# The memory's features through the weight stream, an eight-wide first group, and a first piece in halves

## The chip, the cores and the metric

One of the eight cores of a Trainium2 chip runs the kernel. The metric is device microseconds (us) from launch to end, median of the runs. The core has TensorE (PE, matrix products), VectorE (DVE), ScalarE (ACT) and GpSimd (POOL), which each take their instructions in order, and SyncE (SP), which here issues DMA transfers, in order too. ACT and POOL also issue some transfers. Sums of products build up in eight banks of PSUM.

## What is computed

One decoder layer for 320 tokens (256 of a prompt and 8 x 8 of a second group), width 2048, float32:

```
p = x @ w_in                       # 2048 -> 43 column tiles of 128
u_x, u_gate, u_rwkv = split(p)     # RG-LRU block and RWKV-7 mixer (16 heads of 64, state S)
mix = concat(rg_lru(conv(u_x)) * gelu(u_gate), rwkv7_mix(u_rwkv)) @ w_out
mem_k = mem @ xa_wk ; mem_v = mem @ xa_wv      # 256 memory tokens
x = LN(ALPHA*x + mix)
x = LN(ALPHA*x + softmax((x @ xa_wq) @ mem_k^T) @ mem_v @ xa_wo)
x = LN(ALPHA*x + relu(x @ mlp_w1)**2 @ mlp_w2)
```

mem_k, mem_v and the states of both mixers are outputs as well.

## The kernel before

Every float32 operand is split into a high and a low part (h and l), and a product of a 128x128 weight tile with activations takes three matmuls: h by aH, h by aL, l by aH. One such set is called a triple here. Weights are stored in the order of use, as pieces of 128x1024 float32 (512 KB) with eight weight tiles each. The class `Stream` brings them: `load` issues the DMA of a piece on SP into one of 3 buffers `wraw`, `conv` casts it on ACT into `wh` (4 buffers), and `poll` subtracts on DVE, `wl` = `wraw` - `wh` (4 buffers); when a subtraction is written out, the next load is too. `get(i)` keeps up to three pieces cast ahead.

Activations are split in the same way, one 128-row k-tile at a time, by `Act.put` (one cast on ACT, one subtraction on DVE) into units `u0` to `u7`: even units hold the high parts of four k-tiles, odd ones the low parts. x (16 k-tiles of 128x320) is in u0 to u7 during the input projection. The memory features (16 k-tiles of 128x256) get the same units afterwards, so that a unit of theirs is free only when the last products with the four k-tiles of x in it are done.

`linear` runs a projection over groups of column tiles. In a group that is g tiles wide, a piece holds 8/g k-tiles for each of the g tiles; the groups of w_in (`G_IN`) are one of 4 tiles, then 37 of one, then one of 2. w_in's column tiles come in the order c0 c1 c2 (codes), then r, k, v (RWKV-7), x, g (RG-LRU) of pair 0, of pair 1, and so on to pair 7. After a tile the function `on_win` reads the PSUM bank and may start or end a task. The 8 tasks ("rwkv", i) and the 8 tasks ("lru", i) are Python generators with many small steps. When the program is written, a planner (`Sched`) lays their steps between the triples by a cost model of its own; the order that comes out is fixed. `sch.drain(name)` writes out what is left of a task at once, with the steps of other tasks that come due, and no triples between:

```
elif kind == "x":
    ...
    sch.drain(("lru", i - 1))
    sch.add(lru_task(i, ue), ("lru", i), 1.0)
```

In an RWKV task PE first computes sums for the normalised keys (`t,KM` and `qn,K`). DVE then makes the operands `AR` and `BK` in seven instructions, here called the block (with a reciprocal in it), PE multiplies them (`AR,BK`), DVE masks the result into `GM`, POOL brings `GM` through DMA into `bm`, inverts small triangular matrices in 30 multiplications and additions (`tt`, `Xp`), and sends the result through DMA (`bx`) as `Xn`, which the products `Xn,GM` on PE need. Then come the scan steps with the state (`R`, `UV`, `S`, `XT`).

The memory's features were loaded by SP as 16 transfers of 128 KB (`t<-in_mem`, L1122), three quarters while the last group of w_in runs (the argument `last` of `linear`), the fourth when the projection `wk` has begun. `wk` is in groups of two tiles. After each of its tiles, `on_k` copies PSUM to a buffer on ACT, and POOL issues two stores of it (`mk`, L1132, and `out_mem_k`, L1133).

At the start x_tile loads the k-tiles of x, 160 KB each, on SP, and a piece of w_in after every second one.

Of the kernel before, what the change touches and what calls it, by code (L numbers as in the profile page):

```python
# [119 lines left out]
class Sched:  # L120
# [169 lines left out]
class Stream:  # L290


    def __init__(self, nc, sch, A, tt, raw, hp, lp, srcs, ahead_conv):
        self.nc, self.sch, self.A, self.tt = nc, sch, A, tt
        self.raw, self.hp, self.lp = raw, hp, lp
        self.srcs = srcs
# [20 lines left out]
    def load(self):  # L317
        k = self.n_load
        t = self.raw.tile([128, 1024], F32, name="wraw")
        self.nc.sync.dma_start(t, self.srcs[k])  # L320
        self.r[k] = t
        self.n_load += 1

    def conv(self):
        k = self.n_conv
        t = self.r.pop(k)
        h = self.hp.tile([128, 1024], F32R, name="wh")
        l = self.lp.tile([128, 1024], F32R, name="wl")
        cur, self.sch.cur = self.sch.cur, None
        self.A.copy(h, t)  # L330
        self.sch.cur = cur
        self.pend.append((k, t, h, l, self.sch.free["A"]))
        self.c[k] = (h, l)
        self.n_conv += 1

    def get(self, i):
        while self.n_load < min(len(self.srcs), self.n_low + 3):
            self.load()
        while self.n_conv < min(self.n_load, i + 1 + min(i, self.ac)):
            self.conv()  # L340
        self.poll(i)
        return self.c.pop(i)


def body(ctx, tc, I, O):
# [113 lines left out]
    class Act:  # L459
# [80 lines left out]
    with ExitStack() as mx_ctx:  # L540
# [25 lines left out]
        def tmp(n=NTOK):  # L566
            return tp.tile([128, 348], F32, name="t")[:, :n]
# [106 lines left out]
        def rwkv(p, zr, zk, zv):  # L674
# [140 lines left out]
            for c in range(4):  # L815
# [19 lines left out]
                yield PE_FH  # L835
# [132 lines left out]
        def sample(p, S0, AR, XT, GM, B4, UV, PT, res):  # L968
# [21 lines left out]
            yield PE_HH  # L990
# [741 lines left out]
```

## Time and profile before

| | before |
|---|---|
| median of 3 runs | 2037.86 us (2033.55 to 2039.96) |
| profiled execution, own time | 2038.85 us |
| its span, first to last instruction | 2036.8 us |
| mean granted TensorE clock | 0.985 |
| PE busy | 1978.4 us |
| DVE, ACT, POOL busy | 1056.1, 894.4, 434.1 us |

The input projection runs from 6.65 us to about 460 us of the span, wk from there to about 608 us, the rest is behind. In rows of the timeline the first number is the start in us, the second how long the row's instructions took, "xN" how many there are, and a bracket gives the idle time of that engine just before, with what ended it. The granted clock is a share of TensorE's 2.4 GHz, so 0.5 is the lower of its levels, 1.2 GHz.

### The profile page before, as it was taken

How to read it: one execution, taken by the hardware profiler on the slowest of the kernel's cores; microseconds unless marked ns; L12 is line 12 of the kernel's file. 1: busy time of each engine (PE TensorE's matmuls, PEld its weight loads, DVE VectorE, ACT ScalarE, POOL GpSimd, SP SyncE). 2: the span in 40 equal slices, each digit the busy share in tenths (PEclk: the TensorE clock that was granted, in tenths of full speed). 3: DMA queues.
4: the chain of work that ended last, by engine and by line, in shares of the span. 5: the costliest groups of instructions: out<-in, count | busy, mean ns of one | idle time of the engine just before them, and what ended most of it. 6: DMA issues, size and time to landing. Idle time of an engine off the chain costs nothing.

```text
span 2036.8 us, 38079 instructions
## 1 busy us (share of the span) xinstructions
PE 1978.4 (97%) x15750; PEld 1883.3 (92%) x15750; DVE 1056.1 (52%) x1654; ACT 894.4 (44%) x1464; POOL 434.1 (21%) x661
## 2 busy tenths in 40 slices
PE   7999999988999999999999999999999999999996
PEld 7998888877898999988899999999999999999996
DVE  5676767755545446444476434443444344433444
ACT  5565565555435335544334543334333342234333
POOL 0143023332311345322154310001000010001133
PEclk9999999998999999999999999999999999999998
DMA  7453343344557764787643444444444444444442
GB/s 238 140 154 94 108 119 117 120 125 132 167 184 245 242 215 144 258 316 279 253 144 116 156 154 145 154 147 152 149 151 149 148 153 147 154 146 154 145 149 90
DMA packets 103149, 333.82 MB, mean 164 GB/s; under 512 B 13808, under 2 KB 23824, under 8 KB 102976
## 3 DMA queue, kind: packets, MB, share of 16 engines
q1 hardware_dynamic: 86688, 278.68, 43.1%
q0 software_dynamic: 16288, 52.72, 7.8%
q8 instruction: 123, 2.02, 0.4%
q14 instruction: 50, 0.41, 0.1%
HBM read 315.66 MB, written 15.65 MB: 163 GB/s over the span
## 4 chain that ended last, share of the span: by engine, by line
PE 93%; DMA 2%; DVE 2%; ACT 1%; issue 1%; POOL 1%; SPq 0%; POOLq 0%; ACTq 0%; DVEq 0%
PE ps L284 93%; DMA t<-in_mem 1%; DMA wraw<-in_w_in 1%; POOL u L284 0%; DVE u L284 0%; DVE wl L284 0%; DMA t<-in_x 0%; ACT u L284 0%; ACT wh L284 0%; DVE t L284 0%; POOL r L284 0%; DMA Xn<-bx 0%; DVE S L284 0%; ACT L284 0%; POOL wl L284 0%
## 5 line engine op out<-in xcount | busy, mean ns | idle before, releaser
L284 DVE TENSOR_TENSOR wl<-wraw,wh 128x1024 fp32r<-128x1024 f32 x494 | 612.5, 1243 | 569.3 <-ACT wh L284 568.8
L284 ACT CAST wh<-wraw 128x1024 fp32r<-128x1024 f32 x502 | 525.7, 1048 | 645.5 <-PE ps L284 577.5
L284 PE MATMUL ps<-u,wh 128*128 128x320 f32 (+1 forms) x3424 | 761.6, 313 | 14.1 <-ACT u L284 13.3
L284 PE MATMUL ps<-r,wh 128*128 128x320 f32 x3072 | 680.9, 310 | 2.1 <-ACT r L284 1.8
L284 PEld LDWEIGHTS ps<-u,wh 128*128 128x128 f32 x3424 | 571.6, 191 | 31.2 <-ACT u L284 13.8
L284 PE MATMUL ps<-u,wl 128*128 128x320 f32 (+1 forms) x1712 | 526.4, 307 | 0.0
L284 PEld LDWEIGHTS ps<-r,wh 128*128 128x128 f32 x3072 | 514.8, 188 | 7.0 <-issue 3.8
L284 PE MATMUL ps<-r,wl 128*128 128x320 f32 x1536 | 475.6, 310 | 0.0
L284 PEld LDWEIGHTS ps<-u,wl 128*128 128x128 f32 x1712 | 326.4, 191 | 0.0
L284 PEld LDWEIGHTS ps<-r,wl 128*128 128x128 f32 x1536 | 289.3, 188 | 0.0
L284 PE MATMUL ps<-h,wh 128*128 128x320 f32 x1024 | 225.6, 309 | 0.0
L284 POOL TENSOR_TENSOR r<-r 128x320 f32<-128x320 f32 x64 | 46.0, 721 | 721.0 <-ACT r L284 721.0
L284 PEld LDWEIGHTS ps<-h,wh 128*128 128x128 f32 x1024 | 170.9, 188 | 0.2
L284 PE MATMUL ps<-h,wl 128*128 128x320 f32 x512 | 158.2, 309 | 0.0
L284 DVE TENSOR_TENSOR u<-u,ps 128x320 f32<-128x320 f32 x134 | 61.6, 484 | 80.6 <-PE ps L284 77.9
L284 ACT ACTIVATE r<-ps 128x320 f32<-128x320 f32 x64 | 28.0, 438 | 157.7 <-PE ps L284 157.7
L284 PEld LDWEIGHTS ps<-h,wl 128*128 128x128 f32 x512 | 96.1, 188 | 0.0
L284 POOL TENSOR_TENSOR s<-s,u 128x320 f32<-128x320 f32 x42 | 66.0, 1571 | 91.5 <-DVE u L284 91.1
L284 PE MATMUL ps<-wh,u 128*128 128x512 f32 x256 | 79.9, 391 | 0.0
L284 ACT ACT_TABLE_LOAD x50 | 64.2, 1283 | 9.1 <-DVE mxs L284 7.6
L893 POOL DMA_DIRECT2D bm<-GM x16 | 10.9, 685 | 241.2 <-DVE GM L284 241.2
L284 PEld LDWEIGHTS ps<-wh,u 128*128 128x128 f32 x256 | 48.1, 188 | 10.0
(245 smaller groups left out, 1625.5 us busy)
## 6 DMA issues: line engine op xcount, KB each, us to landing
wraw<-in_w SPq DMA_DIRECT2D x256, 512.0 KB, 3.5
wraw<-in_w_in SPq DMA_DIRECT2D x86, 512.0 KB, 4.0
wraw<-in_wk SPq DMA_DIRECT2D x32, 512.0 KB, 3.7
wraw<-in_wv SPq DMA_DIRECT2D x32, 512.0 KB, 3.9
wraw<-in_w_out SPq DMA_DIRECT2D x32, 512.0 KB, 4.2
kv<-in_cache_k POOLq DMA_DIRECT2D x32, 512.0 KB, 6.7
wraw<-in_wq SPq DMA_DIRECT2D x32, 512.0 KB, 4.6
kv<-in_cache_v POOLq DMA_DIRECT2D x32, 512.0 KB, 9.1
```

What stands on the lines that cost most here:

```text
L284: r = f(*a, **k)
L893: nc.gpsimd.dma_start(blocks(bm[b], h), GM[HS[1 - h], h, :, 0, :])
```

## The change

The first group of w_in is eight tiles wide (c0 to g0), so a piece there holds one k-tile, and the group has all eight PSUM banks. The memory's features come as four pieces of 512 KB through `Stream`, which casts and subtracts them right into the units (`Act.quarter`), in the order quarter 0, quarter 1, wk piece 0, quarters 2 and 3, wk piece 1 and so on. Piece 0 of w_in is loaded as two halves, by ACT's queue and by SP's, and is cast and subtracted in halves; from the second k-tile of x on a piece is loaded after each k-tile, until three are on the way. The stores `mk` and `out_mem_k` are issued by SP. `PE_HH(0)` and `PE_FH(0)` tell the planner that these steps need no new PSUM bank.

```
--- before.py
+++ after.py
@@ -45,7 +45,7 @@
     return g
 
 
-G_IN = _groups(len(WIN_TILES) - 2, 4) + [(len(WIN_TILES) - 2, 2)]
+G_IN = _groups(len(WIN_TILES) - 2, 8) + [(len(WIN_TILES) - 2, 2)]
 G_SQ = _groups(16, 4)
 G_V = [(0, 4), (4, 4), (8, 4), (12, 4)]
 G_1 = _groups(16, 1)
@@ -290,10 +290,11 @@
 class Stream:
 
 
-    def __init__(self, nc, sch, A, tt, raw, hp, lp, srcs, ahead_conv):
+
+    def __init__(self, nc, sch, A, tt, raw, hp, lp, srcs, at, ahead_conv):
         self.nc, self.sch, self.A, self.tt = nc, sch, A, tt
         self.raw, self.hp, self.lp = raw, hp, lp
-        self.srcs = srcs
+        self.srcs, self.at = srcs, at
         self.ac = ahead_conv
         self.n_load = self.n_conv = self.n_low = 0
         self.r, self.c = {}, {}
@@ -317,23 +318,38 @@
     def load(self):
         k = self.n_load
         t = self.raw.tile([128, 1024], F32, name="wraw")
-        self.nc.sync.dma_start(t, self.srcs[k])
+        src = self.srcs[k][0]
+        if k == 0:
+            self.nc.scalar.dma_start(t[:, :512], src[:, :512])
+            self.nc.sync.dma_start(t[:, 512:], src[:, 512:])
+        else:
+            self.nc.sync.dma_start(t, src)
         self.r[k] = t
         self.n_load += 1
 
     def conv(self):
         k = self.n_conv
         t = self.r.pop(k)
-        h = self.hp.tile([128, 1024], F32R, name="wh")
-        l = self.lp.tile([128, 1024], F32R, name="wl")
+        if self.srcs[k][1] is None:
+            h = self.hp.tile([128, 1024], F32R, name="wh")
+            l = self.lp.tile([128, 1024], F32R, name="wl")
+        else:
+            h, l = self.srcs[k][1]()
         cur, self.sch.cur = self.sch.cur, None
-        self.A.copy(h, t)
+        if k == 0:
+            for c in (slice(0, 512), slice(512, 1024)):
+                self.A.copy(h[:, c], t[:, c])
+                self.tt(l[:, c], t[:, c], h[:, c].bitcast(F32), ALU.subtract)
+            self.n_low += 1
+        else:
+            self.A.copy(h, t)
+            self.pend.append((k, t, h, l, self.sch.free["A"]))
         self.sch.cur = cur
-        self.pend.append((k, t, h, l, self.sch.free["A"]))
         self.c[k] = (h, l)
         self.n_conv += 1
 
     def get(self, i):
+        i = self.at[i]
         while self.n_load < min(len(self.srcs), self.n_low + 3):
             self.load()
         while self.n_conv < min(self.n_load, i + 1 + min(i, self.ac)):
@@ -399,15 +415,24 @@
         return E[:, DER[name] + i:DER[name] + i + w]
 
 
-    srcs = []
+    srcs, at = [], []
     base = {}
 
     def reg(key, name, i0, n):
-        base[key] = len(srcs)
-        srcs.extend(I[name][i0 + i] for i in range(n))
+        base[key] = len(at)
+        at.extend(range(len(srcs), len(srcs) + n))
+        srcs.extend((I[name][i0 + i], None) for i in range(n))
 
     reg("w_in", "w_in", 0, 2 * len(WIN_TILES))
-    reg("wk", "wk", 0, 32)
+
+    k0 = len(srcs)
+    base["mem"], base["wk"] = len(at), len(at) + 4
+    at.extend([k0, k0 + 1, k0 + 3, k0 + 4, k0 + 2])
+    for q in (0, 1, None, 2, 3):
+        srcs.append((I["wk"][0], None) if q is None else
+                    (I["mem"][q].rearrange("p a n -> p (a n)"), lambda q=q: Mm.quarter(q)))
+    at.extend(range(len(srcs), len(srcs) + 31))
+    srcs.extend((I["wk"][i], None) for i in range(1, 32))
     reg("wv", "wv", 0, 24)
     reg("w_out", "w_out", 0, 32)
     reg("wv3", "wv", 24, 8)
@@ -417,7 +442,7 @@
     for c in range(4):
         reg(("w1", c), "w1", 32 * c, 32)
         reg(("w2", c), "w2", 32 * c, 32)
-    st = Stream(nc, sch, A, tt, rawp, hp, lp, srcs, 3)
+    st = Stream(nc, sch, A, tt, rawp, hp, lp, srcs, at, 3)
 
     def mm_piece(i, p, g, act, N, ps, after=None):
 
@@ -479,6 +504,10 @@
                 self.H[q] = self.units[2 * q](self.n)
                 self.L[q] = self.units[2 * q + 1](self.n)
             return q, kt % 4
+
+        def quarter(self, q):
+            self._get(4 * q)
+            return (x[q].rearrange("p a n -> p (a n)") for x in (self.H, self.L))
 
         def h(self, kt):
             q, r = self._get(kt)
@@ -572,7 +601,7 @@
             xr[kt] = t = tmp()
             xr["n"] += 1
             nc.sync.dma_start(t, I["x"][kt // 2][:, kt % 2, :])
-            if kt % 2 and st.n_load < 3:
+            if kt and st.n_load < 3:
                 st.load()
             if kt == 7:
                 nc.sync.dma_start(W, I["vecs"][:, 0:NVEC])
@@ -824,7 +853,7 @@
                 if c:
                     ts_ = p2.tile([128, 64], F32, name="ts")
                     A.mul(ts_, S, PT[:, c:c + 1])
-                yield PE_HH
+                yield PE_HH(0)
                 for o in HS:
                     mm(pr[o, 64:128], XT[o, c, :], R[o, :])
                 if c:
@@ -832,7 +861,7 @@
                         mm(po[h, c * 64:c * 64 + 64], S[h, :], AR[h, c, 1, :], True, False)
                 for i, o in enumerate(HS[::-1]):
                     copy(UV[o, c, i, :], pr[o, 64:128])
-                yield PE_FH
+                yield PE_FH(0)
                 for i, h in enumerate(HS):
                     mm(pr[h, 128:192], BT[:, c, 64 * i:64 * i + 64], UV[:, c, i, :])
                 Sn = p2.tile([128, 64], F32, name="S")
@@ -987,7 +1016,7 @@
             copy(R, pr[:, 0:64])
             for h in HS:
                 mm(po[h, 0:64], ident[h, h], RO[h, 1, :], True, False)
-            yield PE_HH
+            yield PE_HH(0)
             for o in HS:
                 mm(pr[o, 64:128], XT[o, 4, :], R[o, :])
             for i, o in enumerate(HS[::-1]):
@@ -1118,19 +1147,18 @@
         lru_load(0)
 
         def mem_prod(kt):
-            t = tmp(NP)
-            nc.sync.dma_start(t, I["mem"][kt // 4][:, kt % 4, :])
-            Mm.put(kt, t)
+            if kt % 4 == 0:
+                st.get(base["mem"] + kt // 4)
 
         Mm = Act(U[0:8], NP, prod=mem_prod)
-        linear("w_in", G_IN, X, NTOK, on_win, lambda kt: Mm.need(kt) if kt % 4 == 3 and kt < 15 else None)
+        linear("w_in", G_IN, X, NTOK, on_win)
 
 
         def on_k(m, ps):
             t = tmp(NP)
             A.copy(t, ps[:, :NP])
-            nc.gpsimd.dma_start(mk[m], t)
-            nc.gpsimd.dma_start(O["mem_k"][m], t)
+            nc.sync.dma_start(mk[m], t)
+            nc.sync.dma_start(O["mem_k"][m], t)
 
         linear("wk", G_WK, Mm, NP, on_k)
         sch.drain()
```

The change moves instructions at three places that matter here. The first is PE at the end of column tile x1 (the twelfth of w_in). Before, triples stand between `qn,K` and `AR,BK` of pair 0; `ps_837` and `ps_938` are column tiles:

```order
L284 MATMUL ps_868<-t_710,KM_104 128x320
L284 MATMUL ps_870<-qn_799,K_77 128x80 x4
L284 MATMUL ps_837<-u4_290,wh_749 128x320
L284 MATMUL ps_837<-u5_291,wh_749 128x320
L284 MATMUL ps_837<-u4_290,wl_750 128x320
...
L284 MATMUL ps_938<-u4_290,wh_838 128x320
L284 MATMUL ps_938<-u5_291,wh_838 128x320
L284 MATMUL ps_938<-u4_290,wl_839 128x320
L284 MATMUL ps_972<-AR_885,BK_882 64x128
L284 MATMUL ps_973<-AR_885,BK_882 64x128
```

After, these are the rows from `qn,K` of pair 0 on; `ps_1059` is the column tile x1, `ps_1309` the next one (r2), and `t_1144,KM` and `qn_1226,K` belong to pair 1:

```order
L284 MATMUL ps_1111<-t_937,KM_104 128x320
L284 MATMUL ps_1113<-qn_1032,K_77 128x80 x4
L284 MATMUL ps_1118<-code_122,lw_867 128x320
L284 MATMUL ps_1059<-u6_528,wh_960 128x320
L284 MATMUL ps_1059<-u7_529,wh_960 128x320
L284 MATMUL ps_1059<-u6_528,wl_961 128x320
...
L284 MATMUL ps_1166<-AR_1129,BK_1126 64x128
L284 MATMUL ps_1167<-AR_1129,BK_1126 64x128
...
L284 MATMUL ps_1198<-t_1079,KM_104 32x80 x4
...
L284 MATMUL ps_1274<-t_1144,KM_104 128x320
L284 MATMUL ps_1276<-qn_1226,K_77 128x80 x4
L284 MATMUL ps_1309<-u0_152,wh_1009 128x320
```

Where 51 rows of triples stood between `qn,K` and `AR,BK`, there are nine matmuls now (three triples), and between `AR,BK` of pair 0 and `qn,K` of pair 1 there are none.

The second place is DVE at the passage from w_in to wk, where the block of pair 6 stands. Before, `wl_6022` is the low part of the fourth piece of wk, the seven rows from `t_5769` to the second `AR` are the block:

```order
L284 TENSOR_TENSOR wl_6022<-wraw_5858,wh_6021 128x1024
L284 SCALAR_TENSOR_TENSOR t_5769<-z_5572,E_79,ps_6061 128x320
L284 TENSOR_TENSOR bv_6079<-z_5729,ps_6059 128x320
L284 SCALAR_TENSOR_TENSOR X2_5847<-t_5846,t_5769 128x320
L284 RECIPROCAL t_5845<-t_5971 128x320
L284 TENSOR_TENSOR BK_6082<-X2_5847,t_5845 128x2x5x64
L284 SCALAR_TENSOR_TENSOR AR_6085<-t_5971,t_5769 128x5x64
L284 TENSOR_TENSOR AR_6085<-t_5971,z_5391 128x5x64
L284 SCALAR_TENSOR_TENSOR S_6118<-ps_5975,PT_4654,ts_5982 128x64
L284 TENSOR_TENSOR wl_6057<-wraw_5934,wh_6056 128x1024
```

After, `u5` and `u7` are the low parts of memory quarters 2 and 3, and `wl_6000` is that of the second piece of wk:

```order
L284 TENSOR_TENSOR u5_5994<-wraw_5808,u4_5993 128x1024
L284 SCALAR_TENSOR_TENSOR t_5766<-z_5523,E_79,ps_6050 128x320
L284 TENSOR_TENSOR bv_6062<-z_5715,ps_6048 128x320
L284 SCALAR_TENSOR_TENSOR X2_5839<-t_5838,t_5766 128x320
L284 RECIPROCAL t_5837<-t_5927 128x320
L284 TENSOR_TENSOR BK_6065<-X2_5839,t_5837 128x2x5x64
L284 SCALAR_TENSOR_TENSOR AR_6068<-t_5927,t_5766 128x5x64
L284 TENSOR_TENSOR AR_6068<-t_5927,z_5361 128x5x64
L284 TENSOR_TENSOR u7_5997<-wraw_5880,u6_5996 128x1024
L284 SCALAR_TENSOR_TENSOR S_6087<-ps_5934,PT_4640,ts_5941 128x64
L284 TENSOR_TENSOR wl_6000<-wraw_5970,wh_5999 128x1024
```

The low part of wk's second piece has moved from ahead of the block to behind it and behind both quarters.

The third place is SP near the end of w_in, with the transfers in the order of issue. Before:

```order
L320 DMA wraw_5651<-in_wk 128x1024
L320 DMA wraw_5687<-in_wk 128x1024
L320 DMA wraw_5788<-in_wk 128x1024
L1013 DMA out_Ss<-S0_5042 128x512
L1122 DMA t_5802<-in_mem 128x256
L1122 DMA t_5808<-in_mem 128x256
L320 DMA wraw_5858<-in_wk 128x1024
L1122 DMA t_5878<-in_mem 128x256
L320 DMA wraw_5934<-in_wk 128x1024
```

After:

```order
L326 DMA wraw_5543<-in_w_in 128x1024
L326 DMA wraw_5618<-in_mem 128x1024
L832 DMA lg_5681<-in_lora 128x256
L834 DMA S0_5683<-in_S0 128x512
L326 DMA wraw_5699<-in_mem 128x1024
L326 DMA wraw_5775<-in_wk 128x1024
L326 DMA wraw_5808<-in_mem 128x1024
L1042 DMA out_Ss<-S0_5036 128x512
L326 DMA wraw_5880<-in_mem 128x1024
L326 DMA wraw_5970<-in_wk 128x1024
```

The sixteen small transfers of the memory's features, which stood behind three pieces of wk, are four pieces now, and two of them stand ahead of the first piece of wk.

## Rows read from the trace of the kernel before

**Rows 1.** The page: busy time, share and instructions of each engine; the chain that ended last.
```profile
PE 1978.4 (97%) x15750; PEld 1883.3 (92%) x15750; DVE 1056.1 (52%) x1654; ACT 894.4 (44%) x1464; POOL 434.1 (21%) x661
...
PE 93%; DMA 2%; DVE 2%; ACT 1%; issue 1%; POOL 1%; SPq 0%; POOLq 0%; ACTq 0%; DVEq 0%
```

**Rows 2.** Timeline of PE, 0 to 545 us: start, duration, instructions, idle before and its releaser.
```profile
7.96 0.64 PE L284 MATMUL ps<-u,wh 128*128 128x320 f32 x1 [0.67 <-DVE u L284]
...
26.99 0.94 PE L284 MATMUL ps<-u,wh 128*128 128x320 f32 x2 [3.38 <-ACT u L284]
...
448.23 0.48 PE L284 MATMUL ps<-R,XT 64*64 64x64 f32 x4 [4.71 <-DVE R L284]
...
456.60 0.33 PE L284 MATMUL ps<-S,AR 64*64 64x64 f32 x4 [1.02 <-DVE S L284]
...
466.37 0.48 PE L284 MATMUL ps<-R,XT 64*64 64x64 f32 x4 [4.17 <-ACT R L284]
...
483.54 1.04 PE L284 MATMUL ps<-u,wh 128*128 128x256 f32 x2 [3.27 <-ACT u L284]
...
533.60 0.48 PE L284 MATMUL ps<-R,XT 64*64 64x64 f32 x4 [3.62 <-DVE R L284]
```

**Rows 3.** Windows of PE: window, length, busy (matmuls), granted clock, DMA share, GB/s.
```profile
27.00:33.00 6.00, 5.89 (x28) 0.72 0.52 170
448.00:452.00 4.00, 3.77 (x21) 0.57 0.21 37
464.00:473.00 9.00, 6.63 (x67) 0.62 0.19 61
482.00:490.00 8.00, 6.46 (x80) 0.57 0.19 59
532.00:541.00 9.00, 7.40 (x121) 0.62 0.32 105
```

**Rows 4.** Timeline of PE: last matmuls of successive triples, in w_in and in wk.
```profile
33.26 0.31 PE L284 MATMUL ps<-u,wl 128*128 128x320 f32 x1
...
33.70 0.31 PE L284 MATMUL ps<-u,wl 128*128 128x320 f32 x1
...
494.55 0.28 PE L284 MATMUL ps<-u,wl 128*128 128x256 f32 x1
...
494.90 0.28 PE L284 MATMUL ps<-u,wl 128*128 128x256 f32 x1
```

**Rows 5.** Timeline of ACT: an early cast, and casts of the memory's features.
```profile
25.53 1.04 ACT L284 CAST wh<-wraw 128x1024 fp32r<-128x1024 f32 x1 [1.75 <-DMA wraw<-in_w_in]
...
445.48 1.44 ACT L284 CAST u<-t 128x256 fp32r<-128x256 f32 x3 [7.19 <-DMA t<-in_mem]
...
483.08 0.76 ACT L284 CAST u<-t 128x256 fp32r<-128x256 f32 x2 [2.21 <-DMA t<-in_mem]
```

**Rows 6.** Timeline of ACT: the read of PSUM after the first group.
```profile
41.97 0.53 ACT L284 ACTIVATE t<-ps,omu 128x320 f32<-128x320 f32 x1 [1.30 <-PE ps L284]
```

**Rows 7.** Timeline of DVE: the block of pair 6 begins, and the subtraction behind it.
```profile
472.43 0.55 DVE L284 SCALAR_TENSOR_TENSOR t<-z,E,ps 128x320 f32<-128x320 f32 x1 [0.33 <-PE ps L284]
...
477.62 1.21 DVE L284 TENSOR_TENSOR wl<-wraw,wh 128x1024 fp32r<-128x1024 f32 x1
```

**Rows 8.** Timeline of PE: pair 0 from qn,K to AR,BK.
```profile
76.71 1.01 PE L284 MATMUL ps<-qn,K 128*128 128x80 f32 x8
...
86.25 1.32 PE L284 MATMUL ps<-AR,BK 64*64 64x128 f32 x40
```

**Rows 9.** Timeline of POOL: the way of pair 0 from bm to Xn.
```profile
89.52 1.42 POOL L893 DMA_DIRECT2D bm<-GM  x2 [85.46 <-DVE GM L284]
...
117.75 1.39 POOL L918 DMA_DIRECT2D Xn<-bx  x2 [3.04 <-DMA bx<-Xp]
```

**Rows 10.** Timeline of POOL: stores of wk tiles inside the inversion of pair 7.
```profile
509.28 0.59 POOL L1132 DMA_DIRECT2D mk<-t  x1 [0.18 <-issue]
...
522.08 0.57 POOL L1132 DMA_DIRECT2D mk<-t  x1 [0.26 <-issue]
```

More of the change, by code (lines that the diff above doesn't have):

```diff
@@ L45, in _groups @@
     return g
-G_IN = _groups(len(WIN_TILES) - 2, 4) + [(len(WIN_TILES) - 2, 2)]
+G_IN = _groups(len(WIN_TILES) - 2, 8) + [(len(WIN_TILES) - 2, 2)]
 G_SQ = _groups(16, 4)
@@ L319, in load @@
         t = self.raw.tile([128, 1024], F32, name="wraw")
-        self.nc.sync.dma_start(t, self.srcs[k])
+        src = self.srcs[k][0]
+        if k == 0:
+            self.nc.scalar.dma_start(t[:, :512], src[:, :512])
+            self.nc.sync.dma_start(t[:, 512:], src[:, 512:])
+        else:
+            self.nc.sync.dma_start(t, src)
         self.r[k] = t
@@ L326, in conv @@
         t = self.r.pop(k)
-        h = self.hp.tile([128, 1024], F32R, name="wh")
-        l = self.lp.tile([128, 1024], F32R, name="wl")
-        cur, self.sch.cur = self.sch.cur, None
-        self.A.copy(h, t)
+        if self.srcs[k][1] is None:
+            h = self.hp.tile([128, 1024], F32R, name="wh")
+            l = self.lp.tile([128, 1024], F32R, name="wl")
+        else:
+            h, l = self.srcs[k][1]()
+        cur, self.sch.cur = self.sch.cur, None
+        if k == 0:
+            for c in (slice(0, 512), slice(512, 1024)):
+                self.A.copy(h[:, c], t[:, c])
+                self.tt(l[:, c], t[:, c], h[:, c].bitcast(F32), ALU.subtract)
+            self.n_low += 1
+        else:
+            self.A.copy(h, t)
+            self.pend.append((k, t, h, l, self.sch.free["A"]))
         self.sch.cur = cur
-        self.pend.append((k, t, h, l, self.sch.free["A"]))
         self.c[k] = (h, l)
@@ L336, in get @@
     def get(self, i):
+        i = self.at[i]
         while self.n_load < min(len(self.srcs), self.n_low + 3):
@@ L399, in der @@
         return E[:, DER[name] + i:DER[name] + i + w]
-    srcs = []
+    srcs, at = [], []
     base = {}
     def reg(key, name, i0, n):
-        base[key] = len(srcs)
-        srcs.extend(I[name][i0 + i] for i in range(n))
+        base[key] = len(at)
+        at.extend(range(len(srcs), len(srcs) + n))
+        srcs.extend((I[name][i0 + i], None) for i in range(n))
     reg("w_in", "w_in", 0, 2 * len(WIN_TILES))
-    reg("wk", "wk", 0, 32)
+    k0 = len(srcs)
+    base["mem"], base["wk"] = len(at), len(at) + 4
+    at.extend([k0, k0 + 1, k0 + 3, k0 + 4, k0 + 2])
+    for q in (0, 1, None, 2, 3):
+        srcs.append((I["wk"][0], None) if q is None else
+                    (I["mem"][q].rearrange("p a n -> p (a n)"), lambda q=q: Mm.quarter(q)))
+    at.extend(range(len(srcs), len(srcs) + 31))
+    srcs.extend((I["wk"][i], None) for i in range(1, 32))
     reg("wv", "wv", 0, 24)
@@ L481, in _get, with quarter @@
             return q, kt % 4
+        def quarter(self, q):
+            self._get(4 * q)
+            return (x[q].rearrange("p a n -> p (a n)") for x in (self.H, self.L))
         def h(self, kt):
@@ L574, in x_tile @@
             nc.sync.dma_start(t, I["x"][kt // 2][:, kt % 2, :])
-            if kt % 2 and st.n_load < 3:
+            if kt and st.n_load < 3:
                 st.load()
@@ L826, in rwkv @@
                     A.mul(ts_, S, PT[:, c:c + 1])
-                yield PE_HH
+                yield PE_HH(0)
                 for o in HS:
@@ L834, in rwkv @@
                     copy(UV[o, c, i, :], pr[o, 64:128])
-                yield PE_FH
+                yield PE_FH(0)
                 for i, h in enumerate(HS):
@@ L989, in sample @@
                 mm(po[h, 0:64], ident[h, h], RO[h, 1, :], True, False)
-            yield PE_HH
+            yield PE_HH(0)
             for o in HS:
@@ L1120, in mem_prod @@
         def mem_prod(kt):
-            t = tmp(NP)
-            nc.sync.dma_start(t, I["mem"][kt // 4][:, kt % 4, :])
-            Mm.put(kt, t)
+            if kt % 4 == 0:
+                st.get(base["mem"] + kt // 4)
         Mm = Act(U[0:8], NP, prod=mem_prod)
-        linear("w_in", G_IN, X, NTOK, on_win, lambda kt: Mm.need(kt) if kt % 4 == 3 and kt < 15 else None)
+        linear("w_in", G_IN, X, NTOK, on_win)
         def on_k(m, ps):
@@ L1131, in on_k @@
             A.copy(t, ps[:, :NP])
-            nc.gpsimd.dma_start(mk[m], t)
-            nc.gpsimd.dma_start(O["mem_k"][m], t)
+            nc.sync.dma_start(mk[m], t)
+            nc.sync.dma_start(O["mem_k"][m], t)
         linear("wk", G_WK, Mm, NP, on_k)
```

6 lines of the change are left out of this document (3 added, 3 removed).

## The prediction

> **What bounds the kernel now.** I read the page first: PE is busy for 1978.4 us, and the chain that ended last is 93% PE [rows 1]. So only two things can be gained: the 58 us in which PE stands idle, and the time in which it runs at the lower clock. I then listed PE's idle times from its timeline. Six larger ones lie where the change acts [rows 2]: one in the first group (3.38 us, until the cast of a k-tile of x), two near the end of w_in (4.71 and 1.02), two at the passage to wk (4.17 and 3.27), one in wk (3.62). Last I read the windows behind them: the granted clock falls to 0.57 to 0.72 there [rows 3], so that every stall costs a second time. I price that as busy time in the window times (1 minus granted clock). From 608 us on, the order of the instructions is the same in both kernels, and I expect no difference there.
>
> **The change, term by term.** Units: a triple of w_in at full clock takes 33.70 - 33.26 = 0.44 us, one of wk 494.90 - 494.55 = 0.35 [rows 4]. A piece (eight triples) is thus 3.5 us of PE in w_in and 2.8 in wk.
>
> (1) *First group.* With four tiles, a piece of 512 KB holds two k-tiles of x (160 KB each): 832 KB for each 3.5 us of PE. With eight tiles it is one k-tile: 672 KB, 19% less. Before, ACT waited 1.75 us for a piece of w_in (its cast began at 25.53, [rows 5]), and the cast of x behind it on ACT let PE wait until 26.99 [rows 2]. With less to fetch per time, I expect this 3.38 to go, and the low clock after it, 5.89 x 0.28 = 1.7 [rows 3]. Of the halves: the cast of a piece takes 1.04 [rows 5], a half thus some 0.52 (estimate), so PE starts about 0.5 earlier, and the wait of 0.67 for the first low part [rows 2] goes too. Together -0.5 - 0.7 - 3.4 - 1.7 = **-6.3**. Bounds: 0 if the transfers stay late, -7 if nothing is left.
>
> A rule speaks against this group. After the group of four, ACT read each bank in 0.53 us, the first after a wait of 1.30 for PE [rows 6]. With eight tiles, all eight banks belong to the group, and the next tile needs the first one back. But the last k-tile ends bank by bank, 0.44 apart, so bank 0 is done 7 x 0.44 = 3.1 us before the group is, against about 0.5 to 1 for its read: no wait. The Trainium skill, page "Perfetto Trace Analysis", section "Matmuls", says that independent groups should rotate through the banks so that the evacuation of one lies beside the matmuls of the next. By the rule taken alone, a group that takes all banks would add the first read, some 1.4 us; by the rows it adds nothing.
> What does move is DVE: the readings of eight tiles stand in one heap ahead of a low part (`wl`): **+1.0** (estimate from the 1.21 of one subtraction, [rows 7]; bounds 0 and 3).
>
> (2) *Memory, end of w_in.* ACT waited 7.19 us for the small transfers of memory and then cast them [rows 5]; `R` of a scan step stood behind that, and PE waited 4.71 for it and 1.02 for `S` [rows 2]. The transfers were issued behind three pieces of wk; now two of them are ahead of wk and go out as the stream has buffers. They no longer come late: -5.7, and the clock of 448 to 452, 3.77 x 0.43 = 1.6 [rows 3]: **-7.3**. ACT's casts of memory must still wait until PE is done with the k-tiles of x in the same units; if that holds ACT as long, the gain is 0.
>
> (3) *Passage to wk.* Gone: 4.17 + 3.27 [rows 2] and the clock, 6.63 x 0.38 = 2.5 and 6.46 x 0.43 = 2.8 [rows 3], together -12.7. New: the low part of wk's second piece now stands behind the block of pair 6, and behind quarters 2 and 3. The block with `S` behind it runs from 472.43 to 477.62, 5.2 us [rows 7]; with quarter 3 (1.2, as one subtraction) and its own 1.21 this low part is ready some 7.6 us after PE's `qn,K`. Of triples and scan steps PE has only about 2 us in that time. It stays idle for about 5.9 (estimate) and runs at the lower clock after it, as before about 2.8. New stall +8.7; sum **-4.0**. Bounds: -12.7 (the low part isn't waited for) and +3 (the quarters come late too).
>
> (4) *Stores off POOL.* Pair 7's inversion held two pairs of stores, at 509.28 and 522.08 [rows 10]: with 0.59 and 0.57 for `mk`, as much again for `out_mem_k`, and the gaps, some 2.9 us of POOL's chain. PE waited 3.62 for `R` behind it [rows 2], and ran 7.40 x 0.38 = 2.8 below full clock [rows 3]. With 2.9 less, some 0.7 of the wait stays: -2.9 - 2.8 = **-5.7**. Bounds: -6.4 and 0 (if `Xn` was held by PE's own steps). On SP the stores stand in order among the loads, and each waits for ACT's copy of its tile; what is queued behind is the next piece of wk. Three pieces ahead are 3 x 2.8 = 8.4 us of cover; I cost this at nothing, and come back to it in the rivals.
>
> (5) *Drain at x1.* This is what I count against the change. ("lru", 0) is added when x0 is read. Before, x0 was a tile of its own, and the drain at x1 came five tiles of 16 k-tiles later, 5 x 7.0 = 35 us of triples. Now x0 is read with the whole group, behind g0, and four tiles (28 us) are left until x1. The planner has not finished the task by then, as the order shows, so the drain writes out its rest and, with it, steps of pairs 0 and 1 without triples between. Before, PE went from `qn,K` at 76.71 to `AR,BK` at 86.25, 9.5 us, filled with triples [rows 8]. Now three triples and two small products stand there (1.8 us with the rest of `qn,K`). DVE's block takes 5.2 [rows 7] from the end of `qn,K`, so PE is idle for about 3.5. `t,KM` of pair 1 then waits for DVE: a low part (1.2), three smaller operations (1.5), four of `GM`, four copies and `qn` of pair 1, some 6.5 in all against 2.4 of PE's products: +3.5. `qn,K` of pair 1 waits another 1.0 for its reciprocal. That is 8 us of idle and some 2 for the clock, as the window at 27 us shows for a stall of half the size [rows 3]: **+10**. Bounds: 0 (the planner's heap hides behind what is left of the piece) and +16 (each wait has a turn on ACT in it too).
>
> (6) *`Xn` of pair 0.* POOL's way from `bm` at 89.52 to the landing of `Xn` (117.75 + 1.39, and about 3 as `bx` took, [rows 9]) is 32.6 us. In the order, `AR,BK` and `Xn,GM` of pair 0 stood 316 rows apart and now stand 244; by their kinds I price that as 41 us of PE and 28.6 (estimates). The stalls of (5) fill most of the difference: **+1.5** (0 to 5). The later drain at x4 I put at a quarter of the 8 idle us of (5) at most, **+1.5** (0 to 4).
>
> Sum: -6.3 + 1.0 - 7.3 - 4.0 - 5.7 + 10 + 1.5 + 1.5 = **-9.3**. Against the profiled execution, 2038.85 us, that is 2029.5; against the median of the three runs, 1 us lower, 2028.6. I say 2029. What this kernel's measurement can tell from no change is 0.3%, 6.1 us: faster is below 2031.7, slower above 2044.
>
> **Rivals.**
> *A, forecast*, 2023 to 2036: 0.50.
> *B, the drains cost nothing*: PE has enough left at x1, or DVE's heap is shorter than the order lets one think. For it: the low parts of three pieces are ready ahead of the block. Against it: PE's rows there hold no triples. Then (5) and the 1.5 of x4 fall away: 2029 - 11.5 = 2017.5. Chance 0.15.
> *C, the gain is eaten* (or the change doesn't do what it says): ACT is held by units of x in place of transfers, so that (2) gives only half (+3.6), and the drain costs 14 (+4): 2029 + 7.6 = 2036.6, within 0.3% of before. For it: the units are the same ones, and ACT takes its work in order. Chance 0.25.
> *D, SP becomes the brake, slower*: at the end of each of the eight groups of wk, SP stands at a store until ACT has copied the tile, and the loads behind it are late. If PE waits 2 us at each group, that is 16: 2045. It decides from (2044 - 2029)/8 = 1.9 us a group on; below that, the cover of 8.4 us has held. Chance 0.10. Against it speaks that the copy on ACT is short and the stores need no data back. Beside it: the Trainium skill, page "DMA: Bandwidth & Descriptors", section "Issuing engines are not separate DMA queues", says that the engine that issues saves only its time of issue, since all transfers share the same 16 DMA engines. By that rule moving the stores gives POOL's 2.9 us and no more, and the trace's 0.59 a store is of that kind; no row here shows a store on SP.
>
> **How the numbers follow.** The time is that of A. Faster than 2031.7 are B and some four fifths of A: 0.55. Within 0.3%: the rest of A, and C: 0.35. Slower: D: 0.10. The range goes from 2018 (B) to 2040 (C with 3 us more); it leaves out D and half of B. A's own range is 2023 to 2036.
>
> **What would show it.** (1) No idle of PE above 1 us before 30 us, granted clock 1 in 27 to 33 us. (2) No idle before `R` some 10 to 15 us ahead of the end of w_in. (3) A wait of PE of 5 to 7 us in wk's second piece, with DVE's `wl` as its releaser, and none for `u`. (4) Pair 7's `R` waited for less than 1.5. (5) At the end of x1 three waits of PE on DVE (`AR` or `BK`, `t`, `qn`), together 6 to 10. The prediction is wrong if the wait of (3) is above 10 or missing, if (5) is missing, or if `wraw` of wk becomes the releaser of PE's waits by way of ACT.

## The result and the profile after

| | before | after |
|---|---|---|
| median of 6 runs | 2035.37 us (2033.55 to 2039.96) | 2025.24 us (2024.55 to 2028.52) |
| profiled execution's span | 2036.8 us | 2022.8 us |
| mean granted clock | 0.985 | 0.990 |

The ratio of the times is 0.9949, with a 95% interval from 0.9936 to 0.9962. The change makes the kernel 10.1 us faster, 0.5%; forecast were 2029 us, 2018 to 2040. The profiled execution of before lay 3.5 us above its median, that of after 0.7 below, so that the spans differ by 14.0 us; some 4 us of that is spread between executions.

The page of after, engines:

```profile
PE 1974.0 (98%) x15750; PEld 1879.5 (93%) x15750; DVE 1051.6 (52%) x1645; ACT 891.2 (44%) x1451; POOL 418.0 (21%) x629
```

PE is busy for 4.4 us less than in [rows 1], with the same 15750 matmuls: a matmul at the higher clock is shorter (from 27 to 33 us 28 matmuls take 5.89 us at 0.72 in [rows 3], 31 take 5.06 at 1.00 here). Idle times of PE in after's timeline, up to 600 us, to be held against [rows 2]; left out are others below 1 us, the longest 0.92 at 203.84 and 0.97 at 433.08, in scan steps:

```profile
27.11 0.94 PE L284 MATMUL ps<-u,wh 128*128 128x320 f32 x2 [0.39 <-ACT u L284]
...
28.77 0.41 PE L284 MATMUL ps<-u,wl 128*128 128x320 f32 x1 [0.72 <-DVE wl L284]
...
103.42 2.39 PE L284 MATMUL ps<-AR,BK 64*64 64x128 f32 x40 [3.00 <-DVE AR L284]
...
110.03 1.12 PE L284 MATMUL ps<-t,KM 128*128 128x320 f32 x2 [2.17 <-DVE t L284]
...
142.27 0.52 PE L284 MATMUL ps<-Xn,GM 16*32 16x16 f32 x40 [0.70 <-DMA Xn<-bx]
...
308.75 0.42 PE L284 MATMUL ps<-u,wl 128*128 128x320 f32 x1 [1.32 <-DVE wl L284]
...
462.08 0.39 PE L284 MATMUL ps<-u,wl 128*128 128x256 f32 x1 [0.94 <-DVE t L284]
...
473.60 0.58 PE L284 MATMUL ps<-u,wl 128*128 128x256 f32 x1 [5.40 <-DVE wl L284]
```

Of the waits in [rows 2], all of which but the first are above 1 us, none is left in its size. New ones have come: `AR,BK` and `t,KM` at the end of x1 (3.00 and 2.17), a low part `wl` in wk's second piece (5.40), and one in w_in (1.32). Windows of PE in after (columns as in [rows 3]):

```profile
27.00:33.00 6.00, 5.06 (x31) 1.00 0.46 154
60.00:97.00 37.00, 37.00 (x252) 1.00 0.39 123
97.00:125.00 28.00, 22.66 (x251) 0.82 0.34 98
443.00:460.74 17.74, 17.28 (x188) 1.00 0.42 126
460.74:480.00 19.26, 12.92 (x142) 0.82 0.37 110
520.00:545.00 25.00, 25.00 (x407) 1.00 0.63 192
```

The clock is full where it had fallen (27 to 33, 443 to 460.74, 520 to 545), and it is at 0.82 over the stretches with the waits at x1 and in wk.

To lay the time out by stretches, I took windows of 4 us over each trace and summed what each loses against a PE that is always busy at full clock: its length minus busy time times granted clock. "430 to wk" ends with the first 128x256 matmul (460.60 us before, 460.74 after), "wk" with the first matmul of the next stage (608.21 and 598.49). The last columns are runs described below.

```
lost us (idle + clock)   before        after         4 tiles      4 tiles, seq   old memory
0 to 60                  10.8 + 1.7     7.6 + 0.0   10.8 + 1.7    10.2 + 2.6     6.4 + 0.0
60 to 130                 0.0 + 0.0     5.3 + 4.4    0.0 + 0.0     0.0 + 0.0     5.4 + 4.0
130 to 190                0.0 + 0.0     0.7 + 0.0    0.0 + 0.0     0.0 + 0.0     0.0 + 0.0
190 to 225                3.4 + 5.5     3.4 + 3.2    3.6 + 5.9     3.4 + 5.7     3.4 + 1.6
225 to 430                3.7 + 0.0     3.2 + 0.0    3.8 + 0.0     3.8 + 0.4     3.5 + 1.7
430 to wk                 5.7 + 1.2     1.4 + 0.0    0.0 + 0.0     0.0 + 1.2     4.6 + 3.2
wk                       11.1 + 8.2     6.7 + 2.7    6.2 + 2.8     5.3 + 0.0     8.0 + 5.4
```

From before to after: -4.9 at the start, +9.7 at x1, +0.7, -2.3, -0.5, -5.5 before wk, -9.9 in wk. The first six terms nearly cancel, to -2.8, and wk begins at 460.74 in place of 460.60; the 2.9 between the two are not in this table, which goes by recorded busy times. About 0.5 of them is order: 40 matmuls `Xn,GM` (0.52 us) stand ahead of wk in after, at 458.00, and inside it before, at 472.72. The table also takes the first 11 us as full clock, where successive triples stand 0.80 us apart and not 0.44. Where the rest lies is not settled. What is left is wk, 137.75 us long in place of 147.61, so that it ends 9.7 us earlier. After wk, the stretches differ by 4.3 us in two traces with the same order of instructions; that is the spread.

### The profile page after: what moved, and what is told of

It reads as the page before. It is cut to its first block, busy times and chain, and to the rows that moved or that the text cites. A ratio compares the mean times of both kernels' runs of the same rounds, so it can differ in the third digit from the quotient of the medians.

```text
span 2022.8 us, 38045 instructions
## 1 busy us (share of the span) xinstructions
PE 1974.0 (98%) x15750; PEld 1879.5 (93%) x15750; DVE 1051.6 (52%) x1645; ACT 891.2 (44%) x1451; POOL 418.0 (21%) x629
## 4 chain that ended last, share of the span: by engine, by line
PE 90%; POOL 2%; DMA 2%; DVE 2%; issue 1%; ACT 1%; SPq 0%; POOLq 0%; ACTq 0%; DVEq 0%
PE ps L284 90%; POOL Xp L284 1%; POOL tt L284 1%; DMA Xn<-bx 1%; DVE wl L284 1%; DMA wraw<-in_w_in 0%; POOL u L284 0%; DVE t L284 0%; DMA Mp<-bm 0%; DVE u L284 0%; DMA t<-in_x 0%; DMA bx<-Xp 0%; DMA bm<-GM 0%; POOL r L284 0%; DVE GM L284 0%
## 5 line engine op out<-in xcount | busy, mean ns | idle before, releaser
L284 DVE TENSOR_TENSOR wl<-wraw,wh 128x1024 fp32r<-128x1024 f32 (+1 forms) x495 | 610.8, 1239 | 568.0 <-ACT wh L284 567.4
L284 ACT CAST wh<-wraw 128x1024 fp32r<-128x1024 f32 (+1 forms) x503 | 525.9, 1047 | 683.0 <-PE ps L284 570.1
L284 PEld LDWEIGHTS ps<-u,wl 128*128 128x128 f32 x1712 | 324.9, 190 | 10.4 <-DVE wl L284 9.2
```

The lines of the kernel that those rows point to most:

```text
L284: r = f(*a, **k)
```

## Experiments

All are edits of the changed kernel. Times are medians; the ratio is to the kernel before, timed on the same chip (2035.84 us for the first four, 2037.12 for the rest). No run takes back `PE_HH(0)` and `PE_FH(0)`, or the earlier loads of the first pieces, by themselves; what these are worth is not known.

**Stores on POOL.**

```
-            nc.sync.dma_start(mk[m], t)
-            nc.sync.dma_start(O["mem_k"][m], t)
+            nc.gpsimd.dma_start(mk[m], t)
+            nc.gpsimd.dma_start(O["mem_k"][m], t)
```

> The changed kernel, but with the stores mk and out_mem_k issued by POOL again. Theory (term 4): the stores lie in POOL's inversion of pair 7, so PE waits some 3.5 us for R in wk again and runs at the lower clock behind it: 5.7 us longer than the changed kernel, 2031 us. Rival: the gain in wk came from the memory's features alone, and the stores were hidden: within 2 us of 2025. Second rival (D): stores on SP held loads up, so with POOL the time falls below 2023.

Measured: 2030.50 us, ratio 0.9980 (0.9971 to 0.9989): slower than the changed kernel. POOL's timeline, with stores inside the inversion of pair 7 and right ahead of its `bx`, and then PE's:

```profile
501.22 0.59 POOL L1160 DMA_DIRECT2D mk<-t  x1 [2.63 <-ACT t L284]
...
515.99 0.58 POOL L1160 DMA_DIRECT2D mk<-t  x1
...
517.14 0.90 POOL L942 DMA_DIRECT2D bx<-Xp  x1
```

```profile
527.37 0.52 PE L284 MATMUL ps<-Xn,GM 16*32 16x16 f32 x40 [2.15 <-DMA Xn<-bx]
```

PE waits for `Xn`, 2.15 us, not 3.62 as in [rows 2]. wk is 141.67 us long against 137.75. Beside the stores' own time, POOL, in order, stands 2.63 us inside the inversion until ACT has copied the tile to be stored; the forecast had no such wait. Term 4 is of the right kind; its size is 3.9 by wk's length in the two traces and 5.3 by the times (6.3 by the ratios), which cannot be told from the 5.7 of the forecast.

**Four tiles.**

```
-G_IN = _groups(len(WIN_TILES) - 2, 8) + [(len(WIN_TILES) - 2, 2)]
+G_IN = _groups(len(WIN_TILES) - 2, 4) + [(len(WIN_TILES) - 2, 2)]
```

> The changed kernel, but with a first group four tiles wide. Theory (terms 1, 5, 6): the wide group gives 5.1 us at the start (idle and clock) and costs some 14 at the drain at x1, with Xn of pair 0, with the heap on DVE and at x4; without it the kernel is 9 us faster than the changed one: 2016 us, with an idle of about 3.4 before 30 us and no wait at the end of x1. Rival: the stall at the drain is only moved to another drain, or is the price of the streams and not of the group: 2025 to 2030.

Measured: 2019.42 us, ratio 0.9926 (0.9913 to 0.9939): faster than the changed kernel, by 5.8 us (4.7 by the ratios) and not by 9. PE's timeline, and windows:

```profile
27.71 1.16 PE L284 MATMUL ps<-u,wh 128*128 128x320 f32 x2 [3.82 <-ACT u L284]
...
463.33 0.50 PE L284 MATMUL ps<-u,wh 128*128 128x256 f32 x2 [3.42 <-ACT wh L284]
```

```profile
0.00:60.00 60.00, 49.15 (x303) 0.97 0.69 228
60.00:130.00 70.00, 70.00 (x586) 1.00 0.44 132
190.00:225.00 35.00, 31.44 (x454) 0.80 0.33 100
```

The idle time of the first group is back (3.82), and from 60 to 130 us PE is always busy at full clock. So the wide group costs more than it gives. Two things keep the difference below 9. From 60 to 190 us the wide group costs 10.4 us by the table, where some 14 were forecast for the whole of it. And from 190 to 225 us, where `on_win` drains ("rwkv", 0) at the tile v3, the narrow group loses 9.5 us and the wide one 6.6 (six other runs with it: 4.3 to 6.4). At the passage to wk PE now waits 3.42 for a cast on ACT, which stood behind the casts of quarters 2 and 3, in place of the 5.40 of after; wk is as long in both (137.60 and 137.75).

**x and g of pair 1 exchanged.**

```
-    WIN_TILES += [("r", _p), ("k", _p), ("v", _p), ("x", _p), ("g", _p)]
+    WIN_TILES += [("r", _p), ("k", _p), ("v", _p)] + ([("g", _p), ("x", _p)] if _p == 1 else [("x", _p), ("g", _p)])
```

> The changed kernel, but with the columns of x and g of pair 1 exchanged in w_in, so that five tiles (35 us) lie between g0 and the drain at x1, as before the change, with the first group still eight wide. Theory: the drain is late enough, AR,BK of pair 0 has triples ahead of it again, and the two waits (3.0 and 2.2 us in the trace of the changed kernel) and the lower clock behind them go: 9 us, 2016 us. Rival: the steps of pairs 0 and 1 are late because the group is wide, and the waits return one tile later: 2023 to 2026.

Measured: 2028.83 us, ratio 0.9970 (0.9959 to 0.9982). The waits return, as the rival has it, but the time lies above its range too. The rows of PE that replace 103.42 and 110.03, and then ACT's reading of the tile x2:

```profile
110.81 0.78 PE L284 MATMUL ps<-t,KM 128*128 128x320 f32 x2 [1.53 <-DVE t L284]
...
120.77 0.42 PE L284 MATMUL ps<-u,wl 128*128 128x320 f32 x1 [3.71 <-DVE wl L284]
...
155.36 0.86 PE L284 MATMUL ps<-XT,Z 32*32 32x32 f32 x20 [1.43 <-DVE Z L284]
...
160.73 0.37 PE L284 MATMUL ps<-K,RO 64*64 64x64 f32 x2 [3.48 <-ACT RO L284]
```

```profile
156.89 0.47 ACT L284 COPY t<-ps 128x256 f32<-128x256 f32 x2
```

`AR,BK` has its triples again and no wait. But the wait comes back as 3.71 for a low part behind pair 1's block, and as 1.43 and 3.48 in steps of the RWKV tasks 40 us later. From 60 to 190 us this kernel loses 18.4 us, the changed one 10.4. The run does not settle whether a later drain is the remedy, since the edit does a second thing: x1 comes one tile later and x2 does not, so only four tiles (r2, k2, v2, x2) lie between pair 1's task and its drain at x2, in place of five. The waits of 1.43 and 3.48 lie on both sides of the reading of x2 at 156.89, with no triples between them, that is at this drain. The same distance of four tiles went with waits at x1 in the changed kernel.

**wk's second piece ahead of quarters 2 and 3.**

```
-    at.extend([k0, k0 + 1, k0 + 3, k0 + 4, k0 + 2])
-    for q in (0, 1, None, 2, 3):
+    at.extend([k0, k0 + 1, k0 + 4, k0 + 5, k0 + 2, k0 + 3])
+    for q in (0, 1, None, None, 2, 3):
...
```

> The changed kernel, but with wk's second piece ahead of the memory's quarters 2 and 3 in the stream, so that its low part stands ahead of the block of pair 6 on DVE. Theory (term 3): PE then has a whole piece more (2.8 us) to do during the block, and the wait of 5.4 us falls to about 2.6, with a shorter time at the lower clock: 2021 to 2022 us. Rival: PE waits for what the block itself makes, or quarter 2 becomes the late one by as much: 2024 to 2026.

Measured: 2025.58 us, ratio 0.9957 (0.9943 to 0.9971), as the changed kernel. PE and DVE there:

```profile
474.23 0.58 PE L284 MATMUL ps<-u,wl 128*128 128x256 f32 x1 [4.69 <-DVE wl L284]
```

```profile
467.88 1.22 DVE L284 TENSOR_TENSOR u<-wraw,u 128x1024 fp32r<-128x1024 f32 x1
...
469.21 1.22 DVE L284 TENSOR_TENSOR u<-wraw,u 128x1024 fp32r<-128x1024 f32 x1
...
470.34 1.90 DVE L284 SCALAR_TENSOR_TENSOR t<-t,W 128x344 f32<-128x344 f32 x4
...
472.95 2.36 DVE L284 TENSOR_TENSOR wl<-wraw,wh 128x1024 fp32r<-128x1024 f32 x2
```

The second piece's wait is gone. The wait of 4.69 is for the third piece's low part, which stands behind both quarters (`u`), four operations of the RG-LRU (1.90) and two copies. The time is the rival's, but neither theory nor rival named this wait.

**Quarters and pieces in turn.**

```
-    at.extend([k0, k0 + 1, k0 + 3, k0 + 4, k0 + 2])
-    for q in (0, 1, None, 2, 3):
+    at.extend([k0, k0 + 1, k0 + 4, k0 + 6, k0 + 2, k0 + 3, k0 + 5])
+    for q in (0, 1, None, None, 2, None, 3):
...
```

> The changed kernel, but with the order of the stream as quarter 0, quarter 1, wk pieces 0 and 1, quarter 2, wk piece 2, quarter 3. In the run with wk's second piece ahead of quarters 2 and 3 PE still waited 4.7 us, one piece later: for the low part of the third piece, which stood on DVE behind quarter 3 (1.2), four operations of the RG-LRU (1.9) and two copies (0.7). Theory: DVE has more to do in these 15 us than PE gives it time for, but what stands ahead of that low part decides; now only quarter 2 and S do, and the wait falls from 4.7 to about 1, with another 1 for quarter 3: 2021 to 2022 us. Rival: DVE's whole load counts, and the wait moves on to the next piece with its size: 2025 us.

Measured: 2022.26 us, ratio 0.9934 (0.9919 to 0.9949). The interval overlaps that of the changed kernel, so the trace must tell. PE's rows:

```profile
469.83 0.38 PE L284 MATMUL ps<-u,wh 128*128 128x256 f32 x1 [0.71 <-DVE u L284]
...
471.16 0.39 PE L284 MATMUL ps<-u,wl 128*128 128x256 f32 x1 [0.94 <-DVE wl L284]
...
476.04 0.39 PE L284 MATMUL ps<-u,wl 128*128 128x256 f32 x1 [0.76 <-DVE wl L284]
```

The one wait of 4.7 has become three, 0.71, 0.94 and 0.76, and wk loses 7.1 us by the table's count, where it loses 9.4 in after and 10.7 with wk's second piece first. The wait at this place was set by the order on DVE, not by DVE's whole load, which is the same in these runs. The gain in time is smaller: two more waits for low parts, 0.86 at 487.75 and 0.90 at 499.77, are not in after, and wk is 136.90 us long against 137.75.

**Four tiles with that order.** 

> Both that seemed to help: a first group of four tiles and the order quarter 0, quarter 1, wk 0 and 1, quarter 2, wk 2, quarter 3. In the run with four tiles PE waited 3.4 us for the cast of wk's second piece, which stood on ACT behind the casts of quarters 2 and 3 (2.0), and 1.1 for its low part. Theory: that cast comes 2 us earlier and its low part 2.4, so that of 3.4 + 1.1 + 1.6 about 3 is left: 2016 us, against 2019.4 with four tiles alone. Rival: ACT stands behind the block of pair 6 anyway and the wait moves to quarter 2: 2019 to 2020.

Measured: 2020.02 us, ratio 0.9918 (0.9902 to 0.9935). PE's rows:

```profile
463.24 0.50 PE L284 MATMUL ps<-u,wh 128*128 128x256 f32 x2 [1.53 <-ACT wh L284]
...
464.50 0.39 PE L284 MATMUL ps<-u,wl 128*128 128x256 f32 x1 [0.76 <-DVE wl L284]
...
478.08 0.38 PE L284 MATMUL ps<-u,wl 128*128 128x256 f32 x1 [1.63 <-DVE wl L284]
```

3.42 + 1.14 became 1.53 + 0.76, the 1.63 stayed, two new waits of 0.61 and 0.76 came at 471.46 and 472.72, and wk is 134.14 us long in place of 137.60; the table has most of that in the clock (0.0 in place of 2.8). The times do not show these 3.5 us against four tiles alone: the medians lie 0.6 apart, the intervals overlap. The time is the rival's, though the wait it named, for quarter 2, is not there. Against the changed kernel this version and the one with four tiles are both faster.

**The old way of the memory's features.**

```
+    reg("wk", "wk", 0, 32)
...
-            if kt % 4 == 0:
-                st.get(base["mem"] + kt // 4)
+            t = tmp(NP)
+            nc.sync.dma_start(t, I["mem"][kt // 4][:, kt % 4, :])
+            Mm.put(kt, t)
...
-        linear("w_in", G_IN, X, NTOK, on_win)
+        linear("w_in", G_IN, X, NTOK, on_win, lambda kt: Mm.need(kt) if kt % 4 == 3 and kt < 15 else None)
```

> The changed kernel, but with the memory's features by sixteen transfers of 128 KB as before the change. Theory (terms 2 and 3): the waits before the end of w_in (4.7 and 1.0) and at the passage to wk (4.2 and 3.3) come back with their lower clock, and the wait of 5.4 on wk's second piece goes: 11 us longer than the changed kernel, 2036 us. Rival: the small transfers were only late because of the order before the change, and with the stores of mk on SP and the wide group they are not: 2023 to 2029.

Measured: 2037.54 us, ratio 1.0009 (0.9998 to 1.0020), no different from before the change. Its waits:

```profile
450.08 0.48 PE L284 MATMUL ps<-S,AR 64*64 64x64 f32 x4 [3.76 <-DVE S L284]
...
467.96 0.77 PE L284 MATMUL ps<-u,wh 128*128 128x256 f32 x2 [3.05 <-DVE qn L284]
...
487.23 1.04 PE L284 MATMUL ps<-u,wh 128*128 128x256 f32 x2 [4.32 <-ACT u L284]
```

They stand at the places of those in [rows 2], in other sizes: 3.76, 3.05, 4.32. wk begins at 464.29 and is 142.70 long. Without the memory in the stream, the rest of the change is worth nothing in sum; this fits the times above, by which the stores give 5.3 and the wide group takes 5.8.

**The first piece whole.**

```
-        if k == 0:
+        if k < 0:
```

(in `load` and in `conv`) 

> The changed kernel, but with the first piece of w_in loaded, cast and subtracted whole. Theory (term 1): PE starts 0.5 us later (at 6.7 in place of 6.2 us) and waits some 0.7 for the first low part: 1.2 us, which the times cannot tell, so the profile decides: 2025 to 2027 us. Rival: nothing, since the transfer of the next pieces sets the pace of the first group in any case: the wait comes a few us later, and the end of the first group is the same.

Measured: 2026.42 us, ratio 0.9952 (0.9938 to 0.9967). PE's start, and ACT's first reading of the first group, in this kernel and then in after:

```profile
6.87 0.64 PE L284 MATMUL ps<-u,wh 128*128 128x320 f32 x1 [6.87 <-ACT u L284]
...
8.17 0.63 PE L284 MATMUL ps<-u,wh 128*128 128x320 f32 x1 [0.67 <-DVE u L284]
```

```profile
64.27 0.52 ACT L284 ACTIVATE t<-ps,omu 128x320 f32<-128x320 f32 x1
```

```profile
64.79 0.52 ACT L284 ACTIVATE t<-ps,omu 128x320 f32<-128x320 f32 x1
```

PE starts 0.66 us later and waits 0.67 for the first low part. Still the group's end is read 0.5 us earlier than in after, whose waits at 27.11 and 28.77 are not there. The five other traces with the halves and the wide group have this reading between 63.33 and 64.52 us, the earliest with the old way of the memory:

```profile
63.33 0.52 ACT L284 ACTIVATE t<-ps,omu 128x320 f32<-128x320 f32 x1
```

So the 64.27 of the whole piece lies inside the spread of the halves, and a gain from them does not show, in the times or in the traces. That the pieces behind them set the pace is a reading of these rows, not shown.

## Why the prediction was right, point by point

The forecast was -9.3, the medians differ by -10.1; the forecast of 2029 started from an earlier, 2.5 us longer median of before. The terms against the table of lost time follow. The measured ones sum to -12.7; with the 2.9 that the table lacks this is the 9.7 us by which wk ends earlier, close to the medians:

| term | forecast | measured |
|---|---|---|
| (1) first group and halves | -6.3 | -4.9 |
| (1) heap on DVE | +1.0 | 0 |
| (2) memory, end of w_in | -7.3 | -5.5 |
| (3) and (4) wk | -9.7 | -9.9 |
| (5) drain at x1 | +10 | +9.7 |
| (6) Xn of pair 0 | +1.5 | +0.7 |
| (6) drain at x4 | +1.5 | -0.5 |
| 190 to 225 us (drain at v3), not priced | | -2.3 |

(1) The 3.38 and the clock behind it went, as forecast. Waits of 0.39 and 0.72 stayed in this trace. The five other traces with the halves and the wide group lose 6.4 to 7.2 us here and not 7.6, so that the term is -4.9 to -6.1. The part of the halves (1.2 of the 6.3) is not borne out by the run with the whole piece. PE is busy for all of 60 to 97 us at full clock, so neither the heap on DVE nor the return of the banks costs anything. ACT reads the group's banks one after the other, from 64.79 us on, beside PE's matmuls. The rule of the Trainium skill, page "Perfetto Trace Analysis", section "Matmuls", that independent groups should rotate through the banks, would taken alone let one expect a bubble here; the trace shows none, though this group holds all eight banks.

(2) ACT's casts of the memory now wait for PE to free the units, as feared, but briefly. The casts in after's timeline of ACT:

```profile
444.75 1.05 ACT L284 CAST u<-wraw 128x1024 fp32r<-128x1024 f32 x1 [0.32 <-PE ps L284]
...
461.31 2.01 ACT L284 CAST u<-wraw 128x1024 fp32r<-128x1024 f32 x2
```

The first waited 0.32 us for PE, where the small transfers made ACT wait 7.19 [rows 5].

(3) The step held in detail. DVE's rows at the place:

```profile
466.01 0.55 DVE L284 SCALAR_TENSOR_TENSOR t<-z,E,ps 128x320 f32<-128x320 f32 x1
...
471.00 1.22 DVE L284 TENSOR_TENSOR u<-wraw,u 128x1024 fp32r<-128x1024 f32 x1
...
472.33 1.21 DVE L284 TENSOR_TENSOR wl<-wraw,wh 128x1024 fp32r<-128x1024 f32 x1
```

The block, quarter 3 (1.22), `S` and the low part (1.21) stand in this order; PE waits 5.40 for it (forecast 5.9) and loses 2.7 by the clock in wk (forecast 2.8). Of the fall in wk, the old way of the memory gives back 5.0 (142.70 against 137.75) and the stores on POOL 3.9; the other microsecond is in neither alone. So by the traces term 4 was sized too high and term 3 too low, since I took the wait for `R` of [rows 2] as the stores' alone: in the run with the stores on POOL PE waits 2.15 there. By the times (5.3) term 4 was not off.

(5) DVE's rows at x1:

```profile
98.20 0.55 DVE L284 SCALAR_TENSOR_TENSOR t<-z,E,ps 128x320 f32<-128x320 f32 x1 [0.18 <-PE ps L284]
...
103.20 1.22 DVE L284 TENSOR_TENSOR wl<-wraw,wh 128x1024 fp32r<-128x1024 f32 x1
...
105.90 1.66 DVE L284 TENSOR_TENSOR GM<-ps,KM 128x512 f32<-128x512 f32 x4
...
109.33 0.55 DVE L284 SCALAR_TENSOR_TENSOR t<-z,W,X 128x320 f32<-128x320 f32 x1 [0.48 <-DVE X L284]
```

PE waited for the end of the block (3.00) and then, behind a low part, `GM` and the copies, for `t` of pair 1 (2.17); `qn,K` waited 0.17 and not 1.0. The idle time is 5.3 and not 8, but the lower clock costs 4.4 and not 2: the window 97 to 125 shows 0.82 over 22.66 busy us. The three waits lie below the 6 to 10 that were to show this term; the sum came out by two errors that cancel, which is luck. Rival B is out, since the waits are there. That the wide group causes them is shown by the run with four tiles. That the four tiles up to the drain do, as I put it, is not shown by itself: the exchange of x and g took these waits away, and the larger ones that it brought lie in part at the next drain, which then came four tiles after its task. This fits term 5 and does not prove it.

(6) `Xn` of pair 0 was waited for 0.70 us at 142.27; at x4 (ACT reads it at 281 us) the longest wait is 0.44 us. The drain at v3 (last row) was not priced. It is more than the spread of one trace: all seven traces with the wide group lose 4.3 to 6.6 us from 190 to 225 us, the three with the narrow one 8.9 to 9.5, nearly all of the difference in the clock (0.0 to 3.3 in place of 5.5 to 5.9). Why the narrow group fares worse there is open.

C is out, since ACT did not hold the memory back and the drain cost 9.7, not 14. D is out: SP's rows in after show how short a store is there, and the load behind it goes out at once:

```profile
485.30 0.33 SPq L1160 DMA_DIRECT2D mk<-t  x1
...
486.15 0.45 SPq L1160 DMA_DIRECT2D mk<-t  x1
...
487.18 1.50 SPq L326 DMA_DIRECT2D wraw<-in_wk  x1
```

A store takes 0.33 to 0.45 us of SP, where POOL needed 0.57 to 0.59 [rows 10], and PE shows no wait above 0.4 us from 480 to 598 us. By the rule of the Trainium skill, page "DMA: Bandwidth & Descriptors", section "Issuing engines are not separate DMA queues", only the time of issue is saved by another engine. For the time that a store itself takes the rows agree, and it counts because it lay in POOL's chain, on which PE waited. What the rule leaves out is the wait ahead of a store: with the stores on POOL this chain also stood 2.63 us for ACT's copy.

## What to carry to other kernels

Look at what stands ahead of an instruction on its own in-order engine, not at the engine's load: here what stood ahead of one subtraction on DVE set a wait of 5.4 us, and another order of the stream left three of under 1 in its place. The same holds for an engine that issues a store: it also waits for what is to be stored. A wider first group relieves the transfers, but ends many tiles at once and starts what depends on them late, so count where too few triples are left beside it. Price each stall of PE with the lower clock behind it: here that took from nothing (0.0 with 5.3, wk with four tiles and the last order) over less than half the idle time (2.7 with 6.7, wk after) to more than all of it (5.5 with 3.4, at 190 us before). When a run moves one thing, look at what moves with it: the exchange of two tiles made one drain later and the next one too early.

## What was not expected of the hardware

With the order of instructions the same up to the end of w_in but for the stream's first piece or its last ones, wk began at 460.74, 459.36, 457.62, 458.31 and 459.07 us in five kernels (after, stores on POOL, wk's second piece first, quarters in turn, whole first piece): a spread of 3 us. From 190 to 430 us the idle time of these five is 6.5 to 8.4 us, while the clock cost 3.2, 3.1, 0.0, 3.3 and 3.1 us. Six waits of PE between 201 and 213 us (in after 0.92, 0.51, 0.33, 0.74, 0.34 and 0.33) agree within 0.13 us in all five; up to 225 us the clock cost 3.2, 1.6, 0.0, 3.3 and 1.5 us. Equal waits can cost 3 us of clock in one execution and nothing in another; why is open.
